# Down products of the last four feed-forward blocks as pairs of output units through seven products, with sums of squares and some low parts made by accumulating transfers

## The chip, the cores and the metric

The kernel runs on one core of one Trainium2 chip. The metric is the device time of one execution in microseconds (us). A difference of under about 2% is not told from no change here.

## The reference, cut to what matters

One layer of a hybrid decoder for 576 tokens (512 of a prompt, 64 of samples) with a model width of 1024. The change touches the end of the feed-forward part and the start of what follows it:

```python
h2 = rms_norm(x, w['g_ffn'][l])
x = x + (silu(h2 @ w['w_ffn_gate'][l]) * (h2 @ w['w_ffn_up'][l])) @ w['w_ffn_down'][l]   # 2816 hidden
h3 = rms_norm(x, w['g_ple'][l])
gate = sigmoid(h3 @ w['w_ple_gate'][l])
emb = p[l] @ w['w_ple_proj'][l]
x = x + gate * emb
y = rms_norm(x, w['g_final'])
```

The 2816 hidden channels are 22 blocks of 128. Everything is float32 in and out.

## The kernel before, in words

Tokens lie along the free axis: `res[k]` holds 128 channels of the residual by 576 tokens, for k from 0 to 7. Each float32 operand of a product is split into a high part, which TensorE's float32r format holds, and a low part, which is the rest. A product of two operands is three matmuls: high by high, high weight by low input, low weight by high input. All matmuls of the stretch that matters are 128x128 by 288 tokens.

**Splitting weights.** `split_piece` (L76) takes a loaded weight (`raw`), casts it on ScalarE to the high part and subtracts on VectorE for the low part. `split_dma` (L81) does it another way: ScalarE casts the high part and writes the negated high part into the low tile (L87), and GpSimd issues a transfer that adds the weight from memory to that tile (L88). `ahead` (L116) chooses between the two by the weight's number in the list `seq`.

**Pairs.** `pair` (L1026) computes two output units (128 channels each) for two halves of the tokens by seven products in place of eight. It needs sums of the two weights (`p_s1`, `p_s2`), five split weight operands A, B, C, D for each pair (`p_a`, `p_d`, `p_b`, `p_hi`, `p_lo`), and split sums of the inputs, the forms B11, B21, B22, S1, S2, U3, U4. Four PSUM banks `ba` to `bd` take the products. ScalarE copies between them (`seed`, and `bc<-bb`, L1080), so the order of a pair is a chain through TensorE and ScalarE. A pair's second half (products U4 and B22) is done inside the next pair, and after the last one by `drain`. The weights of pair n+1 and n+2 are prepared while pair n runs.

The list `pairs` holds the gate and up products of blocks 3 to 21, and the down products of blocks 0 to 17 (`("down", m, c)`, three groups of six blocks). The last four blocks, 18 to 21, are done by plain products after the loop: `ac_split` (L976) splits each block's activation in two, and a loop over the eight output units m runs `mm` (L146), whose 192 matmuls wait for nothing but the weights `w_dn3`. After each unit its result is added to `res[m]` (L1389), `scale_split` (L243) makes the split input `hx3[m]` of the next stage, and `add_square` (L250) squares `res[m]` on ScalarE and adds it to `ssum` on VectorE.

**The stage after it.** A step `e_steps` (L1133) computes the embedding product of `w_ple_proj` by seven products with operands `ea`/`eb`, `eh`/`el`, `chi`/`clo`, `dh`/`dl`. Its steps are placed between the matmuls of the first `gate` units (L1453). At the end of the first gate unit `rms` (L260) splits `ssum` in `sp` tiles and sums it over channels with four matmuls (L274, L275), the norm. Everything after depends on it. TensorE is kept in program order by `in_order`. Every engine takes its instructions in the order that the scheduler wrote down; a wait holds up all that stands behind it on its engine.

Of the kernel before, what the change touches and what calls it, by code (L numbers as in the profile page):

```python
# [15 lines left out]
P = 128  # L16
# [12 lines left out]
def trunk(ctx: ExitStack, tc: tile.TileContext, a, o):  # L29
# [81 lines left out]
    dn0 = len(seq)  # L111
    seq += [a["w_dn3"][i] for i in range(KD // 2)] + [a["w_ple_gate"][m] for m in range(KD)]
    state = {"raw": 0, "split": 0, "use": 0, "lim": out0, "pe": None}
    raws, splits = {}, {}

    def ahead(n_raw, n_split):  # L116
        while state["raw"] < min(n_raw, state["lim"]):
            i = state["raw"]
            raws[i] = raw_load(seq[i], seq[i].shape[-1])
            state["raw"] += 1  # L120
        while state["split"] < min(n_split, state["lim"]):
            i = state["split"]

            kw = dict(pl=es_pool["fq"], tag="z", bufs=2) if i >= len(seq) - 2 else {}
            if plain0 < i < dn0 or i in (dn0 + 1, dn0 + 2) or up0 + 4 <= i < out0 and i % 2:
                kw["src"] = seq[i]
            splits[i] = split(raws.pop(i), seq[i].shape[-1], **kw)
            state["split"] += 1
# [686 lines left out]
    aforms = [{n: [] for n in FORMS} for _ in range(3)]  # L815
    oforms = {n: [] for n in FORMS}
    for (kind, j, c), q in zip(pairs, pr):
        q["W"], q["f"] = {"down": (384, aforms[c]), "out": (256, oforms)}.get(kind, (512, mforms if kind in ("ga", "gb") else forms))
        q["n"] = 1024 if kind == "out" else 2 * q["W"]
        q["K"] = slice(0, q["W"]), slice(q["W"], 2 * q["W"])  # L820
        w = {"down": a["w_dn012"][KD * c:], "ga": W[20:28], "gb": W[28:36], "out": a["w_out"], "gu": a["w_ffn_gate"], "gate": a["w_ffn_gate"], "up": a["w_ffn_up"]}[kind]
        q["j"] = (j + 1, j) if (kind, j) == ("out", KD - 2) else (j, j + 1)
        q["src"] = [w[i] for i in q["j"]] if kind != "gu" else [a["w_ffn_gate"][j], a["w_ffn_up"][j]]
# [148 lines left out]

    def ac_split(j):
        t = gg.pop(j)
        xh, xl = (pl.tile([P, T], F32R, name="a" + tag, tag=tag) for pl, tag in ahl[2 * (j - 18):2 * (j - 17)])
        ac.append((xh, xl))  # L976
        nc.scalar.copy(out=xh, in_=t)
        state["ac"] = tt(out=xl, in0=t, in1=xh.bitcast(F32), op=SUB)

    def evict(n):  # L980
# [40 lines left out]
        else:  # L1021
            for sl, z in ab:
                tt(out=res[j][:, sl], in0=z, in1=res[j][:, sl], op=ADD)
            tt(out=res[j + 1], in0=cz, in1=res[j + 1], op=ADD)

    def pair(n):  # L1026

        q, p = pr[n], pr[n - 1] if n > run[0] else None
        nq = pr[n + 1] if n + 1 < run[1] else None
# [22 lines left out]
        if p:  # L1052
            prod(p["c"], p, "D", 0, "U4", True)
            c21(p)
            prod(p["b"], p, "C", 1, "B22", True)
        else:
            prod(q["d"], q, "B", 0, "S1", False)
# [4 lines left out]
        else:  # L1062
            state["lim"] = len(seq) if run[0] else dn0
            ahead(state["use"] + 2, state["use"] + 1)
            if run[0]:
# [18 lines left out]
        prod(q["a"], q, "A", 1, "B21", True)  # L1084
        if nq:
# [285 lines left out]
    banks.reverse()
    close("bf")
    fq = pool("fq", side="right")
    hx3 = [(fq.tile([P, T], F32R, name=f"h3h{k}"), fq.tile([P, T], F32R, name=f"h3l{k}")) for k in range(KD)]
    ssum = pers.tile([P, T], F32, name="ssum", tag="ssum")
    pzs = [two_banks() for _ in range(2)]
    u = next_unit()
    for i in range(2):
        mm(pzs[i], u, ac, off=512 * i, ks=(0, 1))
    for m in range(KD):  # L1380
        if m < 2:
            pz = pzs[m]
            mm(pz, u, ac, off=512 * m, ks=(2, 3))
        else:
            u = u if m % 2 else next_unit()
            pz = two_banks()
            mm(pz, u, ac, off=512 * (m % 2))
# [156 lines left out]
def lay_out(x):  # L1544
# [64 lines left out]
```

## Time and profile before

| | |
|---|---|
| time, median of 2 runs | 818.68 us (818.62 to 818.74) |
| the profiled execution | 818.62 us, of which 816.9 us are the span in the trace |
| TensorE (PE) busy | 809.2 us, 99% of the span |
| VectorE (DVE) busy | 641.0 us, 78% |
| ScalarE (ACT) busy | 531.7 us, 65% |
| GpSimd (POOL) busy | 102.1 us, 12% |

The profile is one execution. Its own time is 0.06 us under the median, so sums made against it can be read against the median as they stand. 1.7 us of it lie outside the span. The busy shares are means over stages whose limits differ; what the other engines can hide is read from the stage.

### The profile page before, as it was taken

The numbers are of one execution on the slowest core, as the hardware profiler recorded it, in microseconds if no ns is written. First come the engines' busy times: TensorE is split into PE (matmuls) and PEld (weight loads), VectorE is DVE, ScalarE is ACT, GpSimd is POOL, SyncE is SP. The second block draws the span as 40 slices with busy tenths as digits, with TensorE's granted clock in tenths as the row PEclk, the third lists the DMA queues.
The fourth block names the chain that finished last, engine by engine and source line by source line (L and its number), as shares of the span: only waits on it lengthen the run. The fifth ranks groups of instructions, "written<-read, shape, count | busy, mean of one in ns | idle before, by whom it ended". The sixth has DMA issues, their size and how long they took to land.

```text
span 816.9 us, 15290 instructions
## 1 busy us (share of the span) xinstructions
PE 809.2 (99%) x6064; PEld 800.9 (98%) x6064; DVE 641.0 (78%) x1108; ACT 531.7 (65%) x910; POOL 102.1 (12%) x169
## 2 busy tenths in 40 slices
PE   9999999999999999999999999999999999999996
PEld 9999999999999999999999999999999999999996
DVE  7898687864988887678998788777787777987757
ACT  7466446567777776477687667766676666866634
POOL 3202120000011111011011211112211111000000
PEclk9999999999999999999999999999999999999999
DMA  8322133222547666347775787657776578551203
GB/s 296 118 78 79 53 107 106 82 81 86 155 125 168 156 167 161 110 120 169 162 154 126 183 208 188 142 121 191 189 181 149 132 172 195 144 144 64 78 2 116
DMA packets 38903, 111.43 MB, mean 136 GB/s; under 512 B 4913, under 2 KB 9265, under 8 KB 38833
## 3 DMA queue, kind: packets, MB, share of 16 engines
q1 hardware_dynamic: 23712, 74.51, 27.4%
q0 software_dynamic: 12960, 32.77, 24.2%
q10 hardware_dynamic: 2160, 3.19, 1.1%
q8 instruction: 47, 0.77, 0.4%
q14 instruction: 24, 0.19, 0.1%
HBM read 105.46 MB, written 5.00 MB: 135 GB/s over the span
## 4 chain that ended last, share of the span: by engine, by line
PE 97%; DVE 2%; DMA 0%; ACT 0%; DVEq 0%; issue 0%
PE bb L918 7%; PE bb L917 7%; PE bb L919 7%; PE mm L152 6%; PE mm L154 6%; PE mm L156 6%; PE ba L919 5%; PE ba L918 5%; PE ba L917 5%; PE bd L919 2%; PE bd L918 2%; PE bd L917 2%; PE bc L918 2%; PE bc L919 2%; PE bc L917 2%; PE bd L152 1%
## 5 line engine op out<-in xcount | busy, mean ns | idle before, releaser
L152 PE MATMUL mm<-hh,whi 128*128 128x288 f32 x320 | 70.3, 300 | 0.1
L154 PE MATMUL mm<-hl,whi 128*128 128x288 f32 x320 | 69.1, 297 | 0.2 <-DVE hl L314 0.2
L156 PE MATMUL mm<-hh,wlo 128*128 128x288 f32 x320 | 68.6, 296 | 0.0
L78 ACT CAST whi<-raw 128x1024 fp32r<-128x1024 f32 x36 | 37.7, 1046 | 37.9 <-PE mm L154 23.5
L902 DVE TENSOR_TENSOR wlo<-rb,whi 128x1024 fp32r<-128x1024 f32 (+1 forms) x43 | 49.4, 1149 | 11.2 <-ACT whi L897 11.2
L79 DVE TENSOR_TENSOR wlo<-raw,whi 128x1024 fp32r<-128x1024 f32 x36 | 43.9, 1219 | 12.5 <-ACT whi L78 11.9
L152 PEld LDWEIGHTS mm<-hh,whi 128*128 128x128 f32 x320 | 51.7, 189 | 1.1 <-ACT hh L310 0.5
L154 PEld LDWEIGHTS mm<-hl,whi 128*128 128x128 f32 x320 | 51.4, 188 | 0.6 <-DVE hl L314 0.4
L156 PEld LDWEIGHTS mm<-hh,wlo 128*128 128x128 f32 x320 | 51.6, 189 | 0.0
L897 ACT CAST whi<-rb 128x1024 fp32r<-128x1024 f32 (+1 forms) x43 | 42.6, 991 | 10.3 <-PE bb L918 3.3
L902 DVE TENSOR_TENSOR clo<-raw,chi 128x1024 fp32r<-128x1024 f32 (+2 forms) x33 | 36.1, 1093 | 15.9 <-ACT chi L897 15.7
L87 ACT ACTIVATE wlo<-raw 128x1024 fp32r<-128x1024 f32 (+1 forms) x36 | 36.3, 1009 | 14.7 <-PE ba L919 14.7
L87 ACT ACTIVATE dl<-rb 128x512 fp32r<-128x512 f32 (+2 forms) x43 | 25.1, 583 | 29.6 <-PE bc L919 29.6
L1080 ACT ACTIVATE bc<-bb 128x288 f32<-128x288 f32 x39 | 15.4, 395 | 39.0 <-PE bb L919 38.9
L897 ACT CAST chi<-raw 128x1024 fp32r<-128x1024 f32 (+2 forms) x33 | 31.0, 940 | 8.0 <-DVE raw L889 7.9
L883 DVE TENSOR_TENSOR rb<-rb 128x512 f32<-128x512 f32 (+2 forms) x43 | 27.0, 627 | 6.9 <-ACT dh L91 6.9
L927 DVE TENSOR_TENSOR cz<-bc,p 128x288 f32<-128x288 f32 x39 | 17.8, 456 | 14.8 <-PE bc L919 14.5
L924 DVE TENSOR_TENSOR cz<-bb,p 128x288 f32<-128x288 f32 x39 | 17.8, 456 | 14.6 <-PE bb L919 9.4
L91 ACT CAST whi<-raw 128x1024 fp32r<-128x1024 f32 (+1 forms) x29 | 28.5, 981 | 0.0
L918 PE MATMUL bb<-f,chi 128*128 128x288 f32 x88 | 26.0, 295 | 0.0
L918 PE MATMUL ba<-f,whi 128*128 128x288 f32 x88 | 25.9, 295 | 0.0
L919 PE MATMUL bb<-f,clo 128*128 128x288 f32 x88 | 25.9, 295 | 0.0
(906 smaller groups left out, 3292.1 us busy)
## 6 DMA issues: line engine op xcount, KB each, us to landing
raw<-in_w_in SPq DMA_DIRECT2D x25, 512.0 KB, 3.9
wlo<-in_w_ffn_up POOLq DMA_DIRECT2D x12, 512.0 KB, 6.0
wlo<-in_w_ffn_gate POOLq DMA_DIRECT2D x11, 512.0 KB, 5.5
rb<-in_w_ffn_up SPq DMA_DIRECT2D x10, 512.0 KB, 4.5
raw<-in_w_ffn_gate SPq DMA_DIRECT2D x10, 512.0 KB, 4.5
rb<-in_w_ffn_gate SPq DMA_DIRECT2D x9, 512.0 KB, 4.9
raw<-in_w_ffn_up SPq DMA_DIRECT2D x9, 512.0 KB, 5.0
rb<-in_w_dn SPq DMA_DIRECT2D x12, 384.0 KB, 4.1
```

The lines of the kernel that those rows point to most:

```text
L78: nc.scalar.copy(out=hi[:, cs], in_=raw[:, cs])
L79: tt(out=lo[:, cs], in0=raw[:, cs], in1=hi[:, cs].bitcast(F32), op=SUB)
L87: neg = act(lo, raw, AF.Copy, scale=-1.0)
L91: nc.scalar.copy(out=hi, in_=raw)
L152: nc.tensor.matmul(out=out[h], lhsT=wh, rhs=xh[:, h * HT:(h + 1) * HT], start=first, stop=False)
L154: nc.tensor.matmul(out=out[h], lhsT=wh, rhs=xl[:, h * HT:(h + 1) * HT], start=False, stop=False)
L156: i = nc.tensor.matmul(out=out[h], lhsT=wl, rhs=xh[:, h * HT:(h + 1) * HT], start=False, stop=last)
L897: nc.scalar.copy(out=tiles[0][:, 0:w], in_=q[raw][:, 0:w])
L902: tt(out=lo, in0=q[raw][:, 0:w], in1=hi.bitcast(F32), op=SUB)
L917: nc.tensor.matmul(out=out, lhsT=wh, rhs=xh, start=k == 0 and not seeded, stop=False, **kw)
L918: nc.tensor.matmul(out=out, lhsT=wh, rhs=xl, start=False, stop=False, **kw)
L919: i = nc.tensor.matmul(out=out, lhsT=wl, rhs=xh, start=False, stop=k == n - 1, **kw)
```

## The change

The four last blocks' down products become a fourth group of `pairs`, `("down", m, 3)`, with inputs of 256 channels per half (`W` 256) and forms made by the new `last_form`. The first half of the loop runs as before up to the last up pair and is drained; then four more calls of `pair`, and a drain. The first of them splits some products in two so that the forms of blocks 18 and 19 are used before those of blocks 20 and 21. The scaling, splitting and squaring of `res` move into `evict`. The embedding's operands, which were prepared in the last up pair, are now prepared in the last down pair, operand A of it through `split_dma`. The first four units of `w_ple_gate` are split by `split_dma`; `w_dn3` leaves `seq`. `add_square` for `res[1]` to `res[5]` becomes a transfer from on-chip memory that adds `sq` to `ssum`; those for 6 and 7 stay on VectorE.

```diff
-    seq += [a["w_dn3"][i] for i in range(KD // 2)] + [a["w_ple_gate"][m] for m in range(KD)]
+    seq += [a["w_ple_gate"][m] for m in range(KD)]
...
-            if plain0 < i < dn0 or i in (dn0 + 1, dn0 + 2) or up0 + 4 <= i < out0 and i % 2:
+            if plain0 < i < dn0 + 4 or up0 + 4 <= i < out0 and i % 2:
                 kw["src"] = seq[i]
...
         sq = tmp.tile([P, T], F32, name="sq", tag="tb")
         act(sq, res[k], AF.Square)
-        (eng or nc.vector).tensor_tensor(out=ssum, in0=ssum, in1=sq, op=ADD)
+        if eng:
+            nc.gpsimd.dma_start(out=ssum, in_=sq, accum_op=ADD)
+        else:
+            tt(out=ssum, in0=ssum, in1=sq, op=ADD)
...
+    up18, d3 = len(pairs) - 3, len(pairs)
+    pairs += [("down", m, 3) for m in range(0, KD, 2)]
...
-    def ac_split(j):
-        t = gg.pop(j)
-        xh, xl = (pl.tile([P, T], F32R, name="a" + tag, tag=tag) for pl, tag in ahl[2 * (j - 18):2 * (j - 17)])
-        ac.append((xh, xl))
-        nc.scalar.copy(out=xh, in_=t)
-        state["ac"] = tt(out=xl, in0=t, in1=xh.bitcast(F32), op=SUB)
+    def last_form(j):
+        if j == 18:
+            tiles = [pers.tile([P, T], F32R, name="f", tag=tag) for tag in ("hh0", "hl0", "hh1", "hl1", "hh2", "hl2", "hh3")]
+        else:
+            tiles = [x[:, 0:T] for _ in range(2) for x in hi_lo(pl=fq, tag="z", bufs=2)]
+            tiles += [fq.tile([P, T], F32R, name="f", tag=tag) for tag in ("h3l6", "h3h7", "h3l7")]
+        t_form(gg.pop(j), gg.pop(j + 1), tiles, aforms[3], -130 if j == 18 else 0)
...
-            tt(out=res[j + 1], in0=cz, in1=res[j + 1], op=ADD)
+            state["ac"] = tt(out=res[j + 1], in0=cz, in1=res[j + 1], op=ADD)
+            for m in (j, j + 1) if pairs[n][2] == 3 else ():
+                hx3.append([fq.tile([P, T], F32R, name=f"h3{x}{m}", tag=f"h3{x}{m}") for x in "hl"])
+                scale_split(m, g_ple, hx3[m])
+                with tc.high_priority(offset=-60):
+                    add_square(m, m < 6)
...
+        elif n == d3:
+            prod(q["d"], q, "B", 0, "S1", False, (0,))
...
-        prod(q["b"], q, "C", 0, "S2", True)
+        if n == d3:
+            prod(q["b"], q, "C", 0, "S2", True, (0,))
+            prod(q["a"], q, "A", 1, "B21", True)
+            prod(q["b"], q, "C", 0, "S2", True, (1,))
+        else:
+            prod(q["b"], q, "C", 0, "S2", True)
...
-        p_hi(qe, "A", qe["A"], "ra")
-        p_lo(qe, "A", "ra")
+        split_dma(qe["ra"][:, 0:1024], qe["A"], qe["src"][0], True)
...
-    for n in range(*run):
+    for n in range(run[0], d3):
+        pair(n)
+    drain(d3 - 1)
+    close("bf")
+    fq = pool("fq", side="right")
+    hx3 = []
+    ssum = pers.tile([P, T], F32, name="ssum", tag="ssum")
+    last_form(20)
+    for n in range(d3, run[1]):
         pair(n)
     drain(run[1] - 1)
-    for j in (20, 21):
-        ac_split(j)
     e_b()
...
-    u = next_unit()
-    for i in range(2):
-        mm(pzs[i], u, ac, off=512 * i, ks=(0, 1))
-    for m in range(KD):
...
-        for sl, z in zip((H0, H1), pz):
-            tt(out=res[m][:, sl], in0=z, in1=res[m][:, sl], op=ADD)
-        scale_split(m, g_ple, hx3[m])
-        with tc.high_priority(offset=-60):
-            add_square(m)
```

What the written order of ScalarE holds from the end of the last up pair (`bc<-bb` is its copy between banks) to the first scaling of `res` before the change; `chi<-ea` and `eh<-eb` are the embedding's operands:

```order
L1080 ACTIVATE bc<-bb 128x288
L86 CAST whi<-raw 128x1024
L87 ACTIVATE wlo<-raw 128x1024
L931 COPY p_8849<-bd 128x288
L897 CAST chi<-ea 128x1024
L86 CAST whi<-raw 128x1024
L87 ACTIVATE wlo<-raw 128x1024
L897 CAST eh<-eb 128x1024
L977 CAST ahh_8907<-tb 128x576
L977 CAST ahh_8903<-ta 128x576
L246 ACTIVATE h3h_8920<-res_78,C 128x576
```

The same engine after the change, from the copy between banks of the last down pair to the squares that feed transfers; `h3h` are the scaled residuals:

```order
L1099 ACTIVATE bc<-bb 128x288
L86 CAST whi<-raw 128x1024
L87 ACTIVATE wlo<-raw 128x1024
L936 COPY p_9272<-bd 128x288
L902 CAST chi<-ea 128x1024
L86 CAST whi<-raw 128x1024
L87 ACTIVATE wlo<-raw 128x1024
L246 ACTIVATE h3h_9308<-res_84,C 128x576
L246 ACTIVATE h3h_9315<-res_85,C 128x576
L902 CAST eh<-eb 128x1024
L257 ACTIVATE sq<-res_82 128x576
L257 ACTIVATE sq<-res_83 128x576
```

The preparation of the embedding's operand B (`eh`) stood ahead of all scaling of `res`, and stands now behind the last of it; the squares of `res[4]` and `res[5]` stand behind that.

GpSimd before the change, its last transfers:

```order
L88 DMA wlo<-in_w_ffn_up 128x1024
L88 DMA dl<-in_w_ffn_up 128x512
L88 DMA dl<-in_w_ple_proj 128x512
L88 DMA wlo<-in_w_dn 128x1024 x2
L1590 UNCONDITIONAL_BRANCH
```

GpSimd after the change, its last transfers:

```order
L88 DMA dl<-in_w_dn 128x256
L259 DMA ssum<-sq 128x576 x2
L88 DMA wlo<-in_w_ple_gate 128x1024
L88 DMA dl<-in_w_ple_proj 128x512
L259 DMA ssum<-sq 128x576
L88 DMA eb<-in_w_ple_proj 128x1024
L88 DMA wlo<-in_w_ple_gate 128x1024 x2
L259 DMA ssum<-sq 128x576 x2
L88 DMA wlo<-in_w_ple_gate 128x1024
```

The five additions into `ssum` now stand in GpSimd's queue between transfers of weights, in the order in which `res` is finished.

## Rows read from the trace of the kernel before

**Rows 1.** The page: busy time of the engines, and the chain that ended last.

```profile
PE 809.2 (99%) x6064; PEld 800.9 (98%) x6064; DVE 641.0 (78%) x1108; ACT 531.7 (65%) x910; POOL 102.1 (12%) x169
...
PE 97%; DVE 2%; DMA 0%; ACT 0%; DVEq 0%; issue 0%
```

**Rows 2.** Windows: length, then busy us (instructions) of PE, PEld, DVE, ACT, POOL; PEclk.

```profile
718.34:743.93 25.59, 25.59 (x194) 25.59 (x193) 21.77 (x36) 13.91 (x21) 0.35 (x1) 1.00 0.43 119
...
752.03:796.40 44.37, 44.37 (x323) 44.05 (x322) 30.23 (x48) 23.76 (x45) 0.00 (x0) 1.00 0.11 36
```

**Rows 3.** Timeline of PE: start us, us, then the instruction.

```profile
718.34 0.29 PE L152 MATMUL bc<-ahh,whi 128*128 128x288 f32 x1
...
743.93 0.30 PE L1146 MATMUL ba<-pf,ea 128*128 128x288 f32 x1
...
744.60 0.29 PE L1148 MATMUL bd<-pf,el 128*128 128x288 f32 x1
...
751.63 0.30 PE L275 MATMUL bc<-sp,onesr 128*128 128x288 f32 x1
```

**Rows 4.** Timeline of ACT in the last up pair.

```profile
707.41 0.63 ACT L87 ACTIVATE dl<-eb 128x512 fp32r<-128x512 f32 x1 [0.23 <-PE bc L919]
707.95 0.60 ACT L91 CAST dh<-eb 128x512 fp32r<-128x512 f32 x1
...
714.31 0.38 ACT L931 COPY p<-bd 128x288 f32<-128x288 f32 x1
714.59 1.05 ACT L897 CAST chi<-ea 128x1024 fp32r<-128x1024 f32 x1
...
716.48 1.06 ACT L87 ACTIVATE wlo<-raw 128x1024 fp32r<-128x1024 f32 x1
717.44 1.04 ACT L897 CAST eh<-eb 128x1024 fp32r<-128x1024 f32 x1
```

**Rows 5.** Timeline of ACT in an earlier pair of 256-wide products.

```profile
337.02 0.40 ACT L91 CAST dh<-rb 128x256 fp32r<-128x256 f32 x1
337.31 0.78 ACT L246 ACTIVATE hy<-res,C 128x576 fp32r<-128x576 f32 x1
337.99 0.67 ACT L254 ACTIVATE ssum<-res 128x576 f32<-128x576 f32 x1
338.57 0.77 ACT L246 ACTIVATE hy<-res,C 128x576 fp32r<-128x576 f32 x1
```

**Rows 6.** Timeline of DVE: the low part of the embedding's operand B.

```profile
721.30 1.22 DVE L902 TENSOR_TENSOR el<-eb,eh 128x1024 fp32r<-128x1024 f32 x1
```

**Rows 7.** DMA issues of GpSimd's queue: count, KB each, median us to landing.

```profile
dl<-in_w_ffn_gate POOLq DMA_DIRECT2D x9, 256.0 KB, 4.7
...
dl<-in_w_out POOLq DMA_DIRECT2D x4, 128.0 KB, 3.2
...
wlo<-in_w_dn POOLq DMA_DIRECT2D x2, 512.0 KB, 7.0
...
dl<-in_w_ple_proj POOLq DMA_DIRECT2D x1, 256.0 KB, 5.2
```

**Rows 8.** Timelines of ACT and DVE: the last square to the norm's operands.

```profile
746.11 0.67 ACT L257 ACTIVATE sq<-res 128x576 f32<-128x576 f32 x1
...
747.76 0.68 ACT L265 CAST sp<-ssum 128x576 fp32r<-128x576 f32 x1
...
746.98 0.75 DVE L258 TENSOR_TENSOR ssum<-ssum,sq 128x576 f32<-128x576 f32 x1
...
748.47 0.76 DVE L266 TENSOR_TENSOR sp<-ssum,sp 128x576 fp32r<-128x576 f32 x1 [0.74 <-ACT sp L265]
```

**Rows 9.** Windows at the end (columns as in rows 2), and the last matmul.

```profile
809.00:813.00 4.00, 1.62 (x14) 1.30 (x12) 2.82 (x9) 2.83 (x5) 0.00 (x0) 1.00 0.11 44
813.00:817.00 4.00, 0.00 (x0) 0.00 (x0) 0.00 (x0) 0.00 (x0) 0.00 (x0) 0.53 0.58 218
...
810.46 0.27 PE L1529 MATMUL ba<-ident,yg 128*128 128x128 f32 x1
```

More of the change, by code (lines that the diff above doesn't have):

```diff
@@ L814, in trunk @@
     mforms, forms = ({n: [] for n in FORMS} for _ in range(2))
-    aforms = [{n: [] for n in FORMS} for _ in range(3)]
+    aforms = [{n: [] for n in FORMS} for _ in range(4)]
     oforms = {n: [] for n in FORMS}
     for (kind, j, c), q in zip(pairs, pr):
-        q["W"], q["f"] = {"down": (384, aforms[c]), "out": (256, oforms)}.get(kind, (512, mforms if kind in ("ga", "gb") else forms))
+        q["W"], q["f"] = {"down": (256 if c == 3 else 384, aforms[c]), "out": (256, oforms)}.get(kind, (512, mforms if kind in ("ga", "gb") else forms))
         q["n"] = 1024 if kind == "out" else 2 * q["W"]
         q["K"] = slice(0, q["W"]), slice(q["W"], 2 * q["W"])
-        w = {"down": a["w_dn012"][KD * c:], "ga": W[20:28], "gb": W[28:36], "out": a["w_out"], "gu": a["w_ffn_gate"], "gate": a["w_ffn_gate"], "up": a["w_ffn_up"]}[kind]
+        w = {"down": a["w_dn3"] if c == 3 else a["w_dn012"][KD * c:], "ga": W[20:28], "gb": W[28:36], "out": a["w_out"], "gu": a["w_ffn_gate"], "gate": a["w_ffn_gate"], "up": a["w_ffn_up"]}[kind]
         q["j"] = (j + 1, j) if (kind, j) == ("out", KD - 2) else (j, j + 1)
@@ L906, in p_b, with prod @@
         p_lo(q, "B", "rb")
-    def prod(out, q, u, second, name, seeded):
+    def prod(out, q, u, second, name, seeded, ks=None):
         hi, lo = q[u]
@@ L913, in prod @@
         with in_order():
-            for k in range(n):
+            for k in range(n) if ks is None else ks:
                 wh, wl = (w[:, second * q["W"] + k * P:second * q["W"] + (k + 1) * P] for w in (hi, lo))
@@ L1023, in evict @@
                 tt(out=res[j][:, sl], in0=z, in1=res[j][:, sl], op=ADD)
-            tt(out=res[j + 1], in0=cz, in1=res[j + 1], op=ADD)
+            state["ac"] = tt(out=res[j + 1], in0=cz, in1=res[j + 1], op=ADD)
[4 more added lines that the diff above has]
+                    add_square(m, m < 6)
     def pair(n):
-        q, p = pr[n], pr[n - 1] if n > run[0] else None
+        q, p = pr[n], pr[n - 1] if n > run[0] and n != d3 else None
         nq = pr[n + 1] if n + 1 < run[1] else None
@@ L1070, in pair @@
                 p_s2(qe)
-        if run[0] and n + 3 == run[1]:
+        if n == up18:
             qe["p"] = [pers.tile([P, T], F32, name="pn", tag=t) for t in ("ssum", "rn")]
@@ L1083, in pair @@
                 p_hi(nq, "C", [ctile(t) for t in ("hi", "lo")], "ra")
-        prod(q["a"], q, "A", 1, "B21", True)
+        if n != d3:
+            prod(q["a"], q, "A", 1, "B21", True)
+        else:
+            prod(q["d"], q, "B", 0, "S1", False, (1,))
         if nq:
@@ L1104, in pair @@
             ac_form(pairs[n - 1][1])
-        elif pairs[n - 1][0] == "up":
-            for j in (18, 19):
-                ac_split(j)
+        elif n == up18 + 1:
+            last_form(18)
             with tc.issue_after(c5.ins):
@@ L1291, in drain @@
         q = pr[n]
-        ahead(state["use"] + 4, state["use"] + 3)
+        if n + 1 == len(pairs):
+            ahead(state["use"] + 4, state["use"] + 3)
         c22(q)
@@ L1363, in trunk @@
         tt(out=gg[j], in0=g0, in1=tg, op=MULT)
-    for n in range(*run):
+    for n in range(run[0], d3):
[7 more added lines that the diff above has]
+    for n in range(d3, run[1]):
         pair(n)
     drain(run[1] - 1)
-    for j in (20, 21):
-        ac_split(j)
     e_b()
[L1371 to L1376, printed above, removed]
-    u = next_unit()
-    for i in range(2):
-        mm(pzs[i], u, ac, off=512 * i, ks=(0, 1))
-    for m in range(KD):
[L1381 to L1387, printed above, removed]
-        for sl, z in zip((H0, H1), pz):
-            tt(out=res[m][:, sl], in0=z, in1=res[m][:, sl], op=ADD)
-        scale_split(m, g_ple, hx3[m])
-        with tc.high_priority(offset=-60):
-            add_square(m)
     yg = [fq.tile([P, T - TA], F32, name=f"yg{k}") for k in range(KD)]
@@ L1575, in lay_out @@
     d["w_dn012"] = np.concatenate([units(w, 6) for w in six], axis=0)
-    d["w_dn3"] = two(wd[2304:2816])
+    d["w_dn3"] = units(wd[2304:2816].reshape(4, P, 1024)[[0, 2, 1, 3]].reshape(512, 1024), 4)
     d["w_ple_gate"] = units(x["w_ple_gate"][0])
```

## The prediction

> **What bounds the kernel now.** I read the page first: TensorE is busy for 99% of the span and the chain that ended last is TensorE for 97% [rows 1]. So only two things can move the time: fewer matmuls, or a TensorE that waits. Then the windows by stage. In the plain down products and in the stage behind the norm TensorE is busy in every microsecond, at a granted clock of 1.00, the higher of its two levels [rows 2]. ScalarE is busy for 13.91 of the 25.59 us of the down products and VectorE for 21.77 [rows 2]: this stage has room on ScalarE, little on VectorE. Last the timeline of TensorE: the first plain down matmul starts at 718.34, the embedding's first one at 743.93, the matmul that reads `el` at 744.60, and the first that reads the low part of the norm's operand at 751.63 [rows 3]. 192 matmuls in 743.93 - 718.34 = 25.59 us make 0.133 us for each. No matmul waits there, because the operands were made long before: `eh` at 717.44 [rows 4] and `el` at 721.30 [rows 6], 22 us ahead of use.
>
> **The change part by part.**
>
> *Matmuls.* A pair in seven products takes 7 x 2 x 3 = 42 matmuls for two units, four pairs 168, in place of 192. 24 x 0.133 = 3.2 us are removed from an engine that sets the end. That is the whole gain on offer. All I look for now is whether TensorE gets its operands at that pace. From the first new matmul, at 718.34 since nothing ahead of it is removed, to the matmul that reads `el` are 168 + 5 matmuls, so TensorE could read `el` at 718.34 + 173 x 0.133 = 741.3, and the norm's low part 52 matmuls later, at 748.3.
>
> *ScalarE's work before `eh`.* In the order before, the embedding's operands are finished before the down products begin. After the change they are prepared inside them, and the four pairs need split operands too. The written order holds 54 ScalarE instructions from the first pair's copy between banks to the cast `eh`, which the fourth matmul of the embedding waits for. I count them by size and price each by the distance of starts in stretches without idle time: 10 of 1024 wide (both parts of three `w_ple_gate` units, three of the embedding's operands with the negated copy) at 717.44 - 716.48 = 0.96; 12 of 512 wide at 707.95 - 707.41 = 0.54; 12 copies of 288 at 714.59 - 714.31 = 0.28 [rows 4]; 6 of 256 wide at 0.29, 8 scalings of `res` at 0.68, 6 casts and squares of 576 at 0.58 [rows 5]. Sum: 9.6 + 6.5 + 3.4 + 1.7 + 5.4 + 3.5 = 30.1 us. The first of them follows the first product of the new pairs, some 1.5 us behind 718.34 with a half microsecond for the last form. So even with no wait at all `eh` is done at 719.9 + 30.1 = 750.0, where TensorE could use it at 741. ScalarE, at 65% over the span [rows 1], is the bound of this stage.
>
> *ScalarE's waits.* The forms of blocks 20 and 21 are a chain of some ten operations between VectorE and ScalarE, with 18 matmuls (2.4 us) of cover; the copies between banks have little left between them, since a product of two blocks is 6 matmuls (0.8 us) where one of four is 12. I estimate 2.5 us of ScalarE waits (bounds 0 and 4, the latter if each of the four pairs waits 1 us for its copies). `eh` is then done at 752.5. The copy `bc<-bb` of the last pair stands behind much of that work in the same queue, so TensorE waits inside that pair as well; this is the same delay and not added.
>
> *`el`.* It follows `eh` on VectorE: 1.22 [rows 6]. TensorE reads it at about 753.8 in place of 741.3. Without anything else the norm comes 52 x 0.133 = 6.9 us later, at 760.7.
>
> *The sums of squares.* Before, the chain from the last square to the low part `sp` was 748.47 + 0.76 - 746.11 = 3.1 us on two engines [rows 8]. Now each of five additions is a transfer, and each waits until the one before has landed. No row shows a transfer from on-chip memory; the nearest are the weights' accumulating ones on the same queue: 3.2 us for 128 KB, 4.7 and 5.2 for 256 KB, 7.0 for 512 KB [rows 7]. For 288 KB I take 4.8, nearest to 256 KB, with ends 3.2 and 7.0. The first three run beside ScalarE's work. The fourth reads the square of `res[4]`, which stands behind `eh` on ScalarE: ready at 752.5 + 0.6 = 753.1. The fifth waits for the fourth, and the last square reuses a buffer that the fifth transfer reads: 753.1 + 2 x 4.8 = 762.7. Then square 0.6, addition 0.7, cast 0.6, low part 0.7 and hand-overs 0.3 (steps as in [rows 8]): 2.9, so the norm's low part is there at 765.6. That is later than 760.7, so this chain ends last, with TensorE waiting for it.
>
> The Trainium skill (DMA: Bandwidth & Descriptors, section Anatomy of one DMA) gives 2.0 us plus bytes at 436 GB/s for one transfer of this queue, which makes 2.7 us for 288 KB as an estimate; the trace does not agree, since by it 256 KB would take 2.6 and take 5.2 in [rows 7]. By that rule the chain would end at 753.1 + 5.4 + 2.9 = 761.4; this is the second rival.
>
> *The rest.* GpSimd's queue holds the `eb` transfer (operand A, low) behind the third addition. That addition waits for the second one, and so for two landings behind the first square, which is due in the third pair (some 734.5): 734.5 + 2 x 4.8 = 744.1, then `eb` 7.0 at most behind another queued weight: 753, no later than `el`. Its cover is the delay of `eh`; without that delay it would cost up to 10 us by itself. The splits that VectorE loses are off the path and priced at nothing, and so are the loads: SyncE's queue has 4 weights of 512 KB less and 8 of 256 KB more, read ahead while earlier pairs run. Behind the norm nothing changes but one unit's low part; TensorE is busy without a break there [rows 2], so a delay of the norm goes to the end whole.
>
> *Sum.* The norm's low part at 765.6 in place of 751.63: +14.0 us on the profiled execution, whose own time is 818.62: **832.6 us**, 1.7% slower, the gain of 3.2 us contained in it.
>
> **The rivals.**
>
> *The queues keep up (faster or equal).* If ScalarE's order leaves no wait, what remains is 24 matmuls: 818.62 - 3.2 = 815.4. It decides at 741.3: `eh` would have to be ready there, 9 us before ScalarE's sum allows without a wait. For it speaks that the added transfers relieve VectorE. Against it stands the sum of 30.1 us, which rests on counts. 0.08.
>
> *Short transfers.* If a transfer inside the chip takes 3.2 us or less, TensorE's own way (760.7) or the chain (762.4) ends last: 818.62 + 9.1 to 10.8 = 828 to 829.5. For it: these transfers do not read the memory outside; against it: 256 KB at 4.7 and more [rows 7]. 0.17.
>
> *Long transfers, or the lower clock.* If a transfer takes 7.0 because weights are queued ahead of it, the norm is at 770.0: 837.0. The other part of this rival is TensorE's clock: the only fall in the trace is at the end, where the window behind the last matmul at 810.46 shows 0.53 after 1.00 with no matmul in it [rows 9]. I expect TensorE idle for 3 to 4 us in the last pair, at `eh` and at the norm. A matmul of 288 columns at 1.2 GHz needs at least 0.24 us; only what follows the last wait counts, and 30 matmuls there at 0.24 add 30 x 0.11 = 3.3: 835.9. The Trainium skill (TensorE: Matmul & The Clock Gate, Part 1) says that an idle array falls to the lower level and that work brings it back; the trace shows the fall and no return. Both together give 840. 0.30.
>
> *ScalarE is a bound, but by less.* If the pairs' operands are prepared earlier than I place them, `eh` comes 3 to 5 us sooner, all the chain with it: 828 to 830, or 825 if the chain is short as well. 0.10.
>
> **How the numbers follow.** The forecast as worked out has 0.35 (831 to 834.5), and with the others 0.08, 0.17, 0.30 and 0.10. The range 825 to 840 leaves out the rival with the queues that keep up and the worst of long transfers with a low clock, together some 0.15. About 2% (16.4 us, 835.0) is what a measurement of this kernel can tell from no change: slower by over 2% has the larger part of the long-transfer rival and a piece of the forecast's edge, 0.33; faster by over 2% (under 802.2) no mechanism gives, 0.01; within 2% the rest, 0.66.
>
> **What would show it.** In the changed kernel's timeline: matmuls of the new pairs 0.133 apart with gaps before products that read a bank copied by ScalarE; ScalarE without idle time from about the third new pair to `eh`; the `eh` cast at 751 to 753; TensorE waiting at the embedding's fourth and sixth matmul; then two additions into `ssum` in a row on GpSimd's queue, 4.8 us each, and TensorE waiting at the norm until about 765. The windows would show ScalarE at over 90% in this stage, against 54% before, and a granted clock below 1.00 if the lower level matters. I am wrong if `eh` comes before 745, or if the last additions land before TensorE has reached the norm.

## The result, and the profile after

The changed kernel takes 840.5 us (839.35 and 841.59) where the kernel before takes 818.7: a ratio of 1.0265, 95% interval 1.0248 to 1.0282, slower. The forecast was 832.6, with a range of 825 to 840. The profiled execution took 839.35, of which 837.6 us are its span; it is 20.7 us longer than the span before, and the norm's low part stands 20.75 us later (772.38 after 751.63 in [rows 3]). So all of the loss lies between the first new matmul and the norm.

The page of the changed kernel, busy times and the chain that ended last (before: [rows 1]):

```profile
PE 814.6 (97%) x6040; PEld 802.8 (96%) x6040; DVE 649.1 (77%) x1136; ACT 546.7 (65%) x949; POOL 115.8 (14%) x185
...
PE 92%; DMA 3%; DVE 2%; ACT 1%; issue 0%; DVEq 0%; SPq 0%; POOLq 0%; ACTq 0%
```

TensorE fell from 99% to 97% busy and DMA has come into the chain. Windows by stage, columns as in [rows 2]: the four pairs up to the last one's wait, from there to the embedding, to the norm, and behind it.

```profile
718.69:746.39 27.70, 22.40 (x152) 20.13 (x151) 25.50 (x52) 23.87 (x47) 7.75 (x9) 1.00 0.64 145
746.39:758.28 11.89, 4.63 (x21) 4.05 (x21) 7.21 (x10) 8.67 (x11) 4.32 (x5) 0.68 1.07 258
758.28:772.38 14.10, 11.02 (x58) 10.32 (x58) 3.10 (x5) 3.77 (x8) 0.85 (x1) 0.79 0.54 105
772.81:817.10 44.29, 44.29 (x322) 43.98 (x321) 29.16 (x47) 24.72 (x45) 0.88 (x1) 1.00 0.19 48
```

In the second stretch TensorE works 4.63 of 11.89 us, the clock is below 1.00, and the DMA engines are busy all the time. Behind the norm nothing has changed: 322 matmuls in 44.29 us at 1.00, as in [rows 2]. What TensorE waited for, longest first (total, times, longest):

```profile
PE ba L1168 <- DMA eb<-in_w_ple_proj: 7.2, 1, 7.2
PE bb L922 <- ACT bc L1099: 3.1, 1, 3.1
PE bc L277 <- ACT sp L268: 2.3, 1, 2.3
```

Its timeline at these places. `eb` is the low part of the embedding's operand A, `bc L1099` the last pair's copy between banks.

```profile
718.65 0.30 PE L922 MATMUL ba<-f,whi 128*128 128x288 f32 x1
...
746.39 0.40 PE L922 MATMUL bb<-f,whi 128*128 128x288 f32 x1 [3.10 <-ACT bc L1099]
...
758.28 0.61 PE L1168 MATMUL ba<-pf,eb 128*128 128x288 f32 x1 [7.19 <-DMA eb<-in_w_ple_proj]
758.68 0.44 PE L1166 MATMUL bd<-pf,eh 128*128 128x288 f32 x1
758.92 0.44 PE L1167 MATMUL bd<-pf,eh 128*128 128x288 f32 x1
...
772.38 0.40 PE L278 MATMUL bc<-sp,onesr 128*128 128x288 f32 x1 [0.26 <-DVE sp L269]
```

TensorE stands still until 758.28, for `eb` and not for `eh`. Behind the wait matmuls are 0.24 us apart, at the lower level of the clock (1.2 GHz, granted 0.50 from 755 to 764), where those of [rows 2] are 0.133 apart. ScalarE at the same places:

```profile
752.76 1.03 ACT L902 CAST eh<-eb 128x1024 fp32r<-128x1024 f32 x1
753.70 0.68 ACT L257 ACTIVATE sq<-res 128x576 f32<-128x576 f32 x1
755.04 0.68 ACT L257 ACTIVATE sq<-res 128x576 f32<-128x576 f32 x1 [0.67 <-DMA ssum<-sq]
...
765.22 0.69 ACT L257 ACTIVATE sq<-res 128x576 f32<-128x576 f32 x1 [5.12 <-DMA ssum<-sq]
...
769.20 0.68 ACT L257 ACTIVATE sq<-res 128x576 f32<-128x576 f32 x1 [2.67 <-DMA ssum<-sq]
```

`eh` comes within 1.3 us of where the prediction put it (752.5). From there on ScalarE waits, for landings of additions whose source buffers it needs again. GpSimd's queue tells why:

```profile
740.61 0.85 POOL L259 DMA_DIRECT2D ssum<-sq  x1 [4.07 <-PE bb L924]
741.49 0.86 POOL L88 DMA_DIRECT2D wlo<-in_w_ple_gate  x1
742.03 1.21 POOL L88 DMA_DIRECT2D dl<-in_w_ple_proj  x1
747.93 0.86 POOL L259 DMA_DIRECT2D ssum<-sq  x1 [4.69 <-ACT whi L86]
748.46 1.20 POOL L88 DMA_DIRECT2D eb<-in_w_ple_proj  x1
749.00 1.55 POOL L88 DMA_DIRECT2D wlo<-in_w_ple_gate  x1
751.69 0.84 POOL L88 DMA_DIRECT2D wlo<-in_w_ple_gate  x1 [1.14 <-ACT wlo L87]
755.67 0.86 POOL L259 DMA_DIRECT2D ssum<-sq  x1 [3.14 <-DMA ssum<-sq]
765.69 0.85 POOL L259 DMA_DIRECT2D ssum<-sq  x1 [9.16 <-DMA ssum<-sq]
```

The second addition is issued at 740.61 and lands 6.8 us later, at 747.4. The third, which waits for that landing, is issued half a microsecond behind it, at 747.93. (The profile names a ScalarE cast as what ended that wait. The same half microsecond lies between the first landing, 740.05, and the second issue, and between the fourth, 765.13, and the fifth, so I put it down to the landing.) `eb`, whose negated copy ScalarE had finished at 744.71, stands behind that waiting instruction, is issued at 748.46 and lands 9.8 us later. The fourth addition waits for the third (7.0) and takes 9.5 itself, behind `eb` and two gate weights; the fifth, with an empty queue, takes 3.4.

### The profile page after: what moved, and what is told of

The parts are those of the page before. It is cut to its first block, busy times and chain, and to the rows that moved or that the text cites. A ratio compares the mean times of both kernels' runs of the same rounds, so it can differ in the third digit from the quotient of the medians.

```text
span 837.6 us, 15377 instructions
## 1 busy us (share of the span) xinstructions
PE 814.6 (97%) x6040; PEld 802.8 (96%) x6040; DVE 649.1 (77%) x1136; ACT 546.7 (65%) x949; POOL 115.8 (14%) x185
## 4 chain that ended last, share of the span: by engine, by line
PE 92%; DMA 3%; DVE 2%; ACT 1%; issue 0%; DVEq 0%; SPq 0%; POOLq 0%; ACTq 0%
PE bb L922 7%; PE bb L923 7%; PE bb L924 7%; PE mm L152 6%; PE mm L154 6%; PE mm L156 6%; PE ba L924 5%; PE ba L923 5%; PE ba L922 5%; PE bd L923 3%; PE bd L924 3%; PE bd L922 2%; PE bc L923 2%; PE bc L922 2%; PE bc L924 2%; DMA ssum<-sq 2%
## 5 line engine op out<-in xcount | busy, mean ns | idle before, releaser
L907 DVE TENSOR_TENSOR wlo<-rb,whi 128x1024 fp32r<-128x1024 f32 (+2 forms) x47 | 52.2, 1110 | 11.0 <-ACT whi L902 10.8
L78 ACT CAST whi<-raw 128x1024 fp32r<-128x1024 f32 x30 | 31.4, 1046 | 36.8 <-PE mm L154 23.4
L902 ACT CAST whi<-rb 128x1024 fp32r<-128x1024 f32 (+2 forms) x47 | 45.1, 960 | 10.2 <-PE bb L923 4.3
L907 DVE TENSOR_TENSOR clo<-raw,chi 128x1024 fp32r<-128x1024 f32 (+2 forms) x36 | 38.1, 1060 | 16.6 <-ACT chi L902 16.5
L87 ACT ACTIVATE wlo<-raw 128x1024 fp32r<-128x1024 f32 (+2 forms) x41 | 40.3, 983 | 15.9 <-PE ba L924 15.9
L79 DVE TENSOR_TENSOR wlo<-raw,whi 128x1024 fp32r<-128x1024 f32 x30 | 36.6, 1220 | 12.9 <-ACT whi L78 12.5
L87 ACT ACTIVATE dl<-rb 128x512 fp32r<-128x512 f32 (+2 forms) x47 | 26.7, 568 | 30.1 <-PE bc L924 30.0
L1099 ACT ACTIVATE bc<-bb 128x288 f32<-128x288 f32 x43 | 17.0, 395 | 41.8 <-PE bb L924 41.7
L929 DVE TENSOR_TENSOR cz<-bb,p 128x288 f32<-128x288 f32 x43 | 19.6, 456 | 15.7 <-PE bb L924 9.3
L923 PE MATMUL bb<-f,chi 128*128 128x288 f32 x100 | 29.8, 298 | 0.6 <-DVE f L972 0.6
L91 ACT CAST whi<-raw 128x1024 fp32r<-128x1024 f32 (+2 forms) x32 | 30.3, 947 | 0.0
L922 PE MATMUL bb<-f,chi 128*128 128x288 f32 x96 | 28.8, 300 | 0.5 <-DVE cz L929 0.3
L924 PE MATMUL bb<-f,clo 128*128 128x288 f32 x96 | 28.6, 298 | 0.1
```

The source lines that it names most:

```text
L78: nc.scalar.copy(out=hi[:, cs], in_=raw[:, cs])
L79: tt(out=lo[:, cs], in0=raw[:, cs], in1=hi[:, cs].bitcast(F32), op=SUB)
L87: neg = act(lo, raw, AF.Copy, scale=-1.0)
L91: nc.scalar.copy(out=hi, in_=raw)
L902: nc.scalar.copy(out=tiles[0][:, 0:w], in_=q[raw][:, 0:w])
L907: tt(out=lo, in0=q[raw][:, 0:w], in1=hi.bitcast(F32), op=SUB)
```

## The experiments

Each run was timed in turn with the kernel before on the same chip, which took 818.7 to 819.2 us. For each profile I split TensorE's loss from 716 to 780 by the starts in its timeline: a distance that ends with a marked wait counts as wait, less the usual 0.133; a distance of 0.18 to 0.26 without one counts as a slow matmul, with what it is over 0.133 (and how many there are). "Lower clock" is the part of the slow ones that ran while the granted clock was at its lower level; the others, 10 to 18 in a profile with the new pairs, ran at a granted clock of 1.00, most of them right behind a wait. The change's gain of 3.2 is taken off the sum of waits and slow matmuls (not for the sixth run, which has all matmuls of before). In the tenth run the 3.1 us that its added matmuls fill are counted as wait.

| run | time, us | ratio to before | waits | slow matmuls | of these, lower clock | sum less 3.2 | span over 816.9 |
|---|---|---|---|---|---|---|---|
| changed kernel | 840.5 | 1.0265 (1.0248 to 1.0282) | 16.9 | 5.0 (48) | 3.6 (34) | 18.8 | 20.7 |
| 1 no additions by transfer | 832.6 | 1.0171 (1.0155 to 1.0188) | 11.3 | 3.3 (31) | 2.0 (19) | 11.4 | 12.7 |
| 2 the first three only | 835.2 | 1.0198 (1.0181 to 1.0215) | 14.2 | 4.6 (44) | 3.5 (33) | 15.6 | 16.9 |
| 3 additions, no new low parts | 835.0 | 1.0203 (1.0179 to 1.0227) | 15.8 | 5.6 (53) | 4.6 (43) | 18.2 | 19.8 |
| 4 neither | 834.1 | 1.0190 (1.0171 to 1.0208) | 15.1 | 3.4 (32) | 2.3 (22) | 15.3 | 16.0 |
| 5 as 1, gate weights later | 831.3 | 1.0147 (1.0131 to 1.0164) | 10.7 | 4.6 (44) | 3.3 (32) | 12.0 | 12.8 |
| 6 before, with additions | 826.5 | 1.0092 (1.0077 to 1.0107) | 4.5 | 3.2 (30) | 3.2 (30) | 7.7 | 8.4 |
| 7 the last two only | 837.6 | 1.0234 (1.0218 to 1.0250) | 16.2 | 4.9 (46) | 3.4 (32) | 17.8 | 19.5 |
| 8 as 5, embedding later | 830.3 | 1.0140 (1.0125 to 1.0155) | 10.5 | 3.0 (29) | 1.5 (15) | 10.3 | 10.8 |
| 9 as 5, operands first | 834.0 | 1.0175 (1.0156 to 1.0194) | 11.5 | 6.3 (60) | 4.5 (42) | 14.7 | 15.5 |
| 10 as 5, filler matmuls | 829.6 | 1.0127 (1.0111 to 1.0143) | 10.8 | 2.8 (27) | 1.5 (14) | 10.4 | 11.0 |
| 11 pairs by themselves | 827.9 | 1.0102 (1.0084 to 1.0120) | 7.7 | 4.5 (43) | 3.0 (29) | 9.0 | 9.4 |
| 12 as 8, norm first | 829.9 | 1.0131 (1.0112 to 1.0149) | 10.8 | 1.5 (14) | 0 (0) | 9.1 | 9.6 |

The two last columns agree within 2 us in every run, so waits and slow matmuls account for the time; short gaps that no wait marks are the rest. The columns to the right of the ratio are of the profiled execution, which is not always near the median: run 3's took 838.4, run 12's 828.3. In runs 2 and 6 the order of ScalarE and VectorE stays that of the kernel they are compared with up to the embedding (in run 6 but for two neighbours); in runs 1 and 7 some instructions of under 1 us changed places.

**1. No additions by transfer.**

```diff
-                    add_square(m, m < 6)
+                    add_square(m)
```

> All additions into `ssum` are done by VectorE; everything else is the changed kernel's. Theory A (the additions, each waiting for the landing before it, hold up GpSimd's queue and with it the embedding operand's transfer `eb`): without them `eb` is issued when its negated copy is there, some 744.7 in place of 748.5, and lands at 752 to 755. TensorE then waits for `eh` (753.8) and `el` (755.0), and 49 matmuls later, some 20 of them 0.24 us apart, the norm's low part stands at about 762.5 in place of 772.4: 830.6 us. Rival B (the queue and the memory are full of weights, the additions only suffer from that): `eb` still lands at about 758, only the last additions' chain goes, 837 us. Rival C (the lower clock after idle time is the larger part): 834 us.

832.6 us. GpSimd, and TensorE at the embedding:

```profile
744.74 0.86 POOL L88 DMA_DIRECT2D eb<-in_w_ple_proj  x1 [2.14 <-ACT eb L87]
```

```profile
753.09 0.59 PE L1168 MATMUL ba<-pf,eb 128*128 128x288 f32 x1 [2.86 <-DMA eb<-in_w_ple_proj]
...
754.97 0.61 PE L1168 MATMUL bd<-pf,el 128*128 128x288 f32 x1 [0.41 <-DVE el L907]
```

`eb` is issued as soon as it is ready and read 5.2 us earlier. Theory A, with the time 2 us above its figure. `el` is read where I had put it, but the norm's low part follows 9.4 us later (764.33), where I had put 7.5: my own terms, 49 matmuls with 20 of them 0.24 apart, make 8.7. The additions cost 7.9 of the 21.8 us; 14 us have other causes.

**2 and 7. Only the first three, only the last two.** `m < 4` and `4 <= m < 6` in the same line.

> Only the additions of the squares of `res[4]` and `res[5]` go back to VectorE; the first three stay transfers. Theory A: `eb` stays behind the third one and is read at about 758.3 as in the changed kernel; the chain of the two last additions is gone, which spares TensorE its wait of 2.3 us at the norm and 0.8 at the bank copy: norm at about 769, 837 us. If the chain of the last additions alone were the cause, as the prediction had it, the norm would come at 760 to 763: 829 to 831 us.

> The counterpart of the run with the last two on VectorE: of the changed kernel's five additions the first three go back to VectorE, those of `res[4]` and `res[5]` stay transfers. Theory A (the first three hold up `eb`, the last two lengthen the norm's chain, and both queue behind weights): `eb` is read at 753 as with no transfer at all, the two additions wait behind two gate weights and the norm comes at 768 to 770, 836 to 838 us. Rival: if the transfers' price is their own length, 3.4 us each behind the square at 754, the norm comes at 764, no later than TensorE gets there, 833 us.

835.2 and 837.6. In run 2 TensorE reads `eb` at 758.68, as in the changed kernel. In run 7 it reads it at 755.41, 2.3 later than in run 1, and waits 2.3 us at the norm, where run 1 has no wait: the first of the two additions takes 6.9 us behind two gate weights (issues of GpSimd, run 7):

```profile
753.99 0.86 POOL L88 DMA_DIRECT2D wlo<-in_w_ple_gate  x1 [3.04 <-ACT wlo L87]
756.84 0.85 POOL L259 DMA_DIRECT2D ssum<-sq  x1 [1.99 <-ACT sq L257]
764.35 0.86 POOL L259 DMA_DIRECT2D ssum<-sq  x1 [6.66 <-DMA ssum<-sq]
```

Both times are nearer to theory A than to its rivals. The first three cost 2.6 us over run 1 by holding up `eb`, the last two 5.0, most of it by the norm's chain; the sum of 7.6 is near the 7.9 of all five.

**3 and 4. Low parts off GpSimd's queue, with the additions and without.** The conditions for the gate weights and for operand A, in run 4 with the edit of run 1:

```diff
-            if plain0 < i < dn0 + 4 or up0 + 4 <= i < out0 and i % 2:
+            if plain0 < i < dn0 or up0 + 4 <= i < out0 and i % 2:
...
-        split_dma(qe["ra"][:, 0:1024], qe["A"], qe["src"][0], True)
+        p_hi(qe, "A", qe["A"], "ra"); p_lo(qe, "A", "ra")
```

> The low parts of `ea`/`eb` and of the first `w_ple_gate` units are made on VectorE again; the five additions stay transfers. ScalarE has four instructions of 0.96 us less, and the written order now has `eh` ahead of the last scalings of `res`. Theory A (an addition takes 3.4 us when nothing is queued beside it, 7 to 9.5 us only behind weights): the last two land 3.4 us each after about 752.5, norm at 763, 831 us. Rival D (an addition inside the chip takes 7 us by itself): the last lands at 767, norm at 770, 838 us.

> Both undone: no addition by transfer, no new low part by transfer; the seven products for the last down products stay. Theory A: what is left is ScalarE's work inside the four pairs, with `eh` at about 746 and the last pair's bank copy at about 744; TensorE waits 1 to 2 us there and a little at the embedding, norm at 755 to 757: 823 to 825 us. Rival E (ScalarE's work is the cause by itself, as the prediction's largest term had it): `eh` at 750 or later, norm at 760, 828 us or more. If the queues keep up after all: 815 to 817 us.

835.0 and 834.1. The times do not tell theory A from its rivals, since a new wait took the place of the old ones: `cz`, the sum that frees a bank, now stands on VectorE behind low parts that wait for ScalarE, which waits for a gate weight's load. TensorE in run 3, then TensorE and ScalarE in run 4:

```profile
752.11 0.61 PE L922 MATMUL bb<-f,chi 128*128 128x288 f32 x1 [7.32 <-DVE cz L929]
```

```profile
755.71 0.61 PE L922 MATMUL bb<-f,chi 128*128 128x288 f32 x1 [8.07 <-DVE cz L929]
```

```profile
748.76 1.05 ACT L78 CAST whi<-raw 128x1024 fp32r<-128x1024 f32 x1 [2.24 <-DMA raw<-in_w_ple_gate]
```

My 823 to 825 for run 4 was wrong by 10 us: with an edit that changes an instruction's engine, the order of the others changes too. The additions of run 3 had a median of 4.8 us, so they don't take 7 by themselves, though the fourth took 7.6 with no weight in its queue, beside loads of SyncE's queue.

**6. The kernel before with the additions.** `add_square` as in the change, and

```diff
-            add_square(m)
+            add_square(m, m < 6)
```

> The kernel before with one thing changed: the squares of `res[1]` to `res[5]` are added to `ssum` by transfers, in the stretch of the plain down products, where GpSimd's queue carries nothing else and a new square is due every 3.2 us. Theory A (3.4 to 4.9 us for an addition with nothing queued beside it): the fifth lands at 745 to 750, the norm comes 0 to 2 us later, 818.7 to 820.7 us. Rival D (7 us by itself): the fifth lands at 760, 830 us.

826.5 us: +7.7, which neither figure has. Landing times (count, KB each, median us):

```profile
ssum<-sq POOLq DMA_DIRECT2D x5, 288.0 KB, 4.6
```

An addition with nothing queued takes 3.4 to 4.9 us, so theory A is right on its length. But squares are due every 3.2 us and their buffers are two: ScalarE waits at a square, VectorE at the first addition that is its own, and TensorE for a bank copy behind them on ScalarE (ScalarE, VectorE, TensorE):

```profile
747.74 0.68 ACT L257 ACTIVATE sq<-res 128x576 f32<-128x576 f32 x1 [3.74 <-DMA ssum<-sq]
...
749.26 0.39 ACT L1157 ACTIVATE bb<-ba 128x288 f32<-128x288 f32 x1
```

```profile
751.72 0.76 DVE L261 TENSOR_TENSOR ssum<-ssum,sq 128x576 f32<-128x576 f32 x1 [6.86 <-DMA ssum<-sq]
```

```profile
749.71 0.61 PE L1149 MATMUL bb<-pf,chi 128*128 128x288 f32 x1 [3.21 <-ACT bb L1157]
```

Thus the additions cost 7.7 us without any of the new products. I had priced the last landing alone, and not who stands behind the instruction that waits for one.

**5. Gate weights later.** Run 1, and

```diff
-            if plain0 < i < dn0 + 4 or up0 + 4 <= i < out0 and i % 2:
+            if plain0 < i < dn0 + 1 or up0 + 4 <= i < out0 and i % 2:
...
-            ahead(state["use"] + 3, state["use"] + 2)
+            ahead(state["use"] + 3, state["use"] + 1)
...
-            ahead(state["use"] + 4, state["use"] + 3)
+            ahead(state["use"] + 4, state["use"] + 1)
```

> As the run with all additions on VectorE (832.6 us), and the second and third `w_ple_gate` units are split later and on VectorE: four ScalarE instructions of 0.96 us leave the stretch before `eh`, which the written order now has right behind the last pair's bank copies, at about 747 in place of 752.6. Theory A (TensorE's late start on the embedding is set by whatever comes last of `eb`'s transfer and of ScalarE's `eh`): `eb` becomes the last, read at 752 to 753 as there; 831 to 832 us. Rival E (ScalarE's work alone sets it): TensorE goes on at about 749, 827 us.

831.3 us, theory A: with 3.8 us of ScalarE work out of the way, `eb` alone is last. It is read at 754.84 and not at 752 to 753, as it is issued 1.7 us later than in run 1 (746.44). The intervals of runs 1 and 5 overlap, so no gain is shown.

**10. Filler matmuls.** Run 5, and 24 matmuls on an idle bank ahead of the one that waits for `eb`:

```diff
+                for _ in range(24 if (i, u, name) == (0, "A", "B11") else 0):
+                    nc.tensor.matmul(out=t["c"], lhsT=wh, rhs=xh, start=True, stop=True)
```

> As the run with the gate weights later (831.3 us), with 24 matmuls more whose product nobody reads, placed where TensorE waits 4 us for `eb`. They take 3.2 us of that wait. Theory (the 0.24 us pitch behind a wait is the lower clock after idle time): some 25 matmuls behind the wait run at 0.133 and the time falls by 2 to 2.7 us, to 829 us, with 24 matmuls more. Rival (the pitch there comes from operands or loads, not from the idle array): 831 us, or more by the added matmuls.

TensorE in run 5, and in run 10:

```profile
754.84 0.61 PE L1168 MATMUL ba<-pf,eb 128*128 128x288 f32 x1 [3.66 <-DMA eb<-in_w_ple_proj]
755.24 0.44 PE L1166 MATMUL bd<-pf,eh 128*128 128x288 f32 x1
755.48 0.44 PE L1167 MATMUL bd<-pf,eh 128*128 128x288 f32 x1
```

```profile
750.91 3.36 PE L1169 MATMUL bc<-pf,ea 128*128 128x288 f32 x24
755.00 0.40 PE L1170 MATMUL ba<-pf,eb 128*128 128x288 f32 x1 [0.72 <-DMA eb<-in_w_ple_proj]
755.23 0.29 PE L1166 MATMUL bd<-pf,eh 128*128 128x288 f32 x1
755.37 0.29 PE L1167 MATMUL bd<-pf,eh 128*128 128x288 f32 x1
```

`eb` comes no earlier, and from the second one on the matmuls behind it are 0.133 apart in place of 0.24. The granted clock shows why (length, PE busy, clock, DMA share, GB/s; run 5, then run 10):

```profile
755.00:758.00 3.00, 3.00 (x13) 0.50 0.00 0
```

```profile
755.00:758.00 3.00, 3.00 (x22) 1.00 0.03 5
```

829.6 us after 831.3, though with 24 matmuls more: 1.7 us, as the 17 fewer slow matmuls give (4.6 to 2.8). The two intervals overlap, so the clock and the distances show the mechanism and the time only agrees with it.

**8 and 12. The embedding one gate unit later.** Run 5, with the operands of the embedding prepared behind the last pair and its steps moved; in run 12 the norm's operands ahead of `clo`, `el`, and one split later (shown is part of run 8's edit; run 12 has `(norm, e_b)`):

```diff
-    e0 = next(E[0])
+    nb = [bank("a"), bank("b")]
...
-    four = [gate("cd", ((sE[0],), (sE[0],), (sE[0], norm), ()))]
+    four = [gate("cd", ((), (), (), (e_b, norm)))]
...
-    four.append(gate("ab", ((), (sE[1],), (sE[1],), (sE[1],))))
+    four.append(gate("ab", ((sE[0],), (sE[0],), (sE[0],), (sE[0],))))
```

> A candidate: the seven products stay, additions on VectorE, second and third gate weights later, and the embedding product starts one gate unit later, so that its operands are prepared beside the first gate unit; the norm's matmuls stand at the end of the first gate unit, on banks of their own, the last squares ahead of weights. Work per engine is as in the run with the later gate weights. Theory (what costs is that operands of the embedding are due where ScalarE has no room): TensorE's waits shrink to those at the first pair (2.6 us), 1 to 2 us at the last pair's bank copy and 2 to 4 us at the norm: 821 to 823 us. If ScalarE's sum is what counts, wherever the work stands: 827 us or more.

> As the run with the embedding one unit later (830.3 us), with the norm's operands ahead of `clo`, `el` and the third gate unit's weight in the written order. There TensorE waited 3.2 us for the norm's low part behind 4.5 us of weight and operand work on VectorE. Theory: that wait shrinks to under 1 us, `el` comes later instead: 827 to 829 us.

830.3 and 829.9. TensorE's longest wait in each:

```profile
759.67 0.40 PE L278 MATMUL ba<-sp,onesr 128*128 128x288 f32 x1 [2.88 <-DVE sp L269]
```

```profile
762.56 0.40 PE L1163 MATMUL bd<-pf,el 128*128 128x288 f32 x1 [3.09 <-DVE el L907]
```

Run 8 missed its 821 to 823: the wait for `eb` became one for the norm's low part, which stood on VectorE behind 4.5 us of weights and operands. Run 12 took that away and got the same wait for `el`, which there stands on VectorE behind the norm's two reciprocals (3.8 us), so its 827 to 829 failed too. There VectorE is the late one, not ScalarE.

**9. Operands first.** Run 5, low part of A on VectorE as in run 3, `cz`, `eh`, `el` ahead in the order, and one gate weight split later (shown is the line that moves `eh` and `el`):

```diff
-    e_b()
+    with tc.high_priority(offset=250): e_b()
```

> From the run with the gate weights later (831.3 us): the low part of `ea`/`eb` is made on VectorE, so that no transfer stands ahead of the embedding, and the written order puts the sums of the last pair (`cz`) and `eh`, `el` ahead of other work on VectorE and ScalarE. Work per engine changes by one subtraction of 1.2 us on VectorE and one copy of 1.0 us less on ScalarE. Theory (after the additions, the embedding's operands set the time by where they stand in the queues): TensorE waits 1 to 2 us at the last pair's bank copy, `el` is there at 750 to 751, norm at 757: 823 to 826 us. If the ScalarE work itself is the bound, 829 us or more.

834.0 us, above run 5, though the two intervals touch. No marked wait of TensorE is over 0.8 us up to the norm (there 2.6), but there are eleven of them, and 60 matmuls are slow, the most of all runs, 42 of them at the lower clock. My theory that the place of the operands is all failed; nor does it speak for ScalarE's sum alone, since the waits are for both engines.

**11. The pairs by themselves.** Run 9, without making operands B, C and D (and without its later split); the line that puts A in their places:

```diff
+                qe.update({x: qe["A"] for x in "BCD"})
```

> As the run with the operands first, but the embedding's operands B, C and D are not prepared: operand A stands in their places, so the output of that product is not the reference's; all matmuls stay. It shows the pairs by themselves. Theory: what is left are the waits inside the four pairs (2.6 us in the first, some 1 us in each of the others), which the gain of 3.2 us in matmuls does not outweigh: 820 to 822 us. If the pairs cost nothing by themselves: 815 to 817 us.

827.9 us. Two of the rows inside the fourth pair, and the norm:

```profile
741.09 0.40 PE L922 MATMUL bb<-f,chi 128*128 128x288 f32 x1 [0.86 <-ACT chi L902]
742.44 0.40 PE L924 MATMUL bb<-f,clo 128*128 128x288 f32 x1 [0.82 <-DVE clo L907]
...
758.65 0.40 PE L277 MATMUL bc<-sp,onesr 128*128 128x288 f32 x1 [1.70 <-ACT sp L268]
```

The waits inside the pairs sum to 5.0 us (2.3 in the first, 2.7 in the others), 2.8 stand at a gate weight and the norm, and 43 slow matmuls cost 4.5, of which 26 with 2.7 lie inside the pairs. Even here 12.2 us are lost for 3.2 gained, 7.7 of them inside the pairs. The pairs still share the engines with the splits of the gate weights and of operand A, so their own price is not shown apart from that. I had 820 to 822, with the waits and without the slow matmuls.

## Why the prediction was wrong

*The step that failed* is a size: "For 288 KB I take 4.8". The nearest rows were those of a queue that is nearly empty. Alone 4.8 is right (median 4.6 in run 6). In the changed kernel the five took 4.5, 6.8, 7.0, 9.5 and 3.4 us to land, and the next one was issued 0.5 to 0.7 us behind a landing. Beside the second, third and fourth, weights of 256 and 512 KB were under way in the same queue and loads in SyncE's. Which of the two stretches them is open: run 3's fourth took 7.6 with loads of SyncE's queue alone. The rival with 7.0 named queued weights as the cause but put it at the last two only; its 14.0 for these is near the measured 13.4, though by luck: they are 9.5, 0.5 and 3.4. The chain as predicted: fourth addition issued at 753.1, two landings of 4.8, then 2.9, norm at 765.6. Measured: issued at 755.67, 2.6 late (half of it because its square was done at 754.38, the rest because the third had only landed at 754.9); 13.4 us to the fifth landing in place of 9.6 (3.8); 3.3 behind it (0.4). Together 6.8, which is the whole miss of the norm (772.4); the median is 1.1 above the profiled execution.

*`eb`* was put at 753 "no later than `el`" (its own terms, 744.1 and 7.0, make 751.1); it was read at 758.28. The same error twice: the third addition came 3.8 us later than reckoned (747.93 for 744.1), and `eb` took 9.8 for 7.0. The prediction allowed it "up to 10 us by itself" and hid it behind the delay of `eh` and `el`; it came 3.2 us after `el` (755.05) and cost TensorE 7.2 us. Run 2, which has this wait and not the norm's chain, still takes 835.2, so a right size for the last two additions would not have been enough; runs 2 and 7 show that the two are separate terms.

*Right:* the gain of 3.2 us (nothing behind the norm changed); no wait in the plain products before; ScalarE's 30.1 us and its waits (`eh` done at 753.8 for 752.5, ScalarE without idle time from 729 on; `el` at 755.05 for 753.8); the wait at the last pair's bank copy as the same delay.

*The lower clock* was a rival priced only behind the last wait, with 30 matmuls; there one was slow. In the changed kernel 34 matmuls ran at the lower level (3.6 us), all of them ahead of waits that cover part of it. Once those waits are gone it is on the path, and run 10 takes part of it away. Without additions the prediction's terms give 760.7 for the norm, 827.7 us; in run 1's profile (831.35 us, 1.2 under the median) its low part is read at 764.33. Of the 3.6 us between, 1.2 are `el` (read at 754.97 for 753.8) and 2.0 the 19 matmuls at the lower level behind it.

*What stays open:* how the 14 us that remain without additions divide between ScalarE's work, `eb` and the pairs' own waits, since each run that took one away brought another; how much of runs 3 and 4 is the new wait on VectorE alone; a written order with both the old order and the other engine wasn't tried. No version that ran beats the kernel before.

## What to carry to other kernels

An accumulating transfer in place of a vector addition is not free because its engine is idle: it holds its queue, its source buffer and everything behind the next instruction that waits for its landing, so price it with what is under way in that queue and the others at that moment. A stage that has no wait at all, as the plain products here, can lose more than twice the removed work when it is cut into dependent pieces of 0.8 us (run 11: 7.7 us inside the pairs for 3.2). Short waits cost more than their length: the matmul behind one is mostly late by another 0.1 us at full clock, and in six of the twelve profiles with the new pairs the clock fell after waits of under 1 us.

## What was not expected of the hardware

The same first pair, with the same waits of 0.6 to 0.9 us at 719 to 724, ran at full clock in seven of the twelve profiles with the new pairs, and at the lower level in five. Windows 723.50 to 727.50 of the changed kernel and of run 5 (length, PE busy, clock, DMA share, GB/s):

```profile
723.50:727.50 4.00, 3.59 (x24) 1.00 0.10 16
```

```profile
723.50:727.50 4.00, 3.79 (x18) 0.72 0.16 12
```

The wait for `cz` in the third pair follows at 733.4 to 733.7 in the one group and at 734.8 to 735.0 in the other. So the same instructions differ by 1.5 us, counted from the first wait of the first pair, and comparisons of single profiles carry that. The Trainium skill (TensorE: Matmul & The Clock Gate, Part 1) says that one kernel measures different counts of matmuls at the lower level at its start, from run to run; these profiles show the like in the middle of one.

Not every slow matmul is the lower clock. Run 12 has 14 of them, most right behind a wait, and its granted clock over the whole stretch is 1.00 (columns as above):

```profile
718.00:776.00 58.00, 48.62 (x344) 1.00 0.49 125
```

For a transfer of 288 KB on GpSimd's queue the Trainium skill (DMA: Bandwidth & Descriptors, Anatomy of one DMA) has a fit that makes 2.7 us as an estimate; no run agrees: 3.4 us is the least, 4.6 the median with nothing queued, 9.5 the most.
